# First MLP of a diffusion block: one sum on DVE placed two units later, and eight narrow matmuls of the mixer's shift spread through the next chunk

## The chip, the cores and the metric

The kernel runs on one core of a Trainium2 chip. The metric is the device time of the program in microseconds (us); the kernel before takes 1244.91 us, the median of 3 runs (1244.38 to 1244.93). The engines of the core are named as in the profile: PE (matmuls), PEld (its weight loads), DVE (vector), ACT (scalar, activations), POOL (GpSimd) and SP (the queue that issues all loads and stores).

## What is computed

Two layers of a diffusion backbone, over 512 latent tokens and 256 context tokens, 1024 wide. Layer 0 mixes tokens with pooling windows, layer 1 with attention; each is followed by an MLP with squared ReLU, 4096 wide. Every sublayer is shifted, scaled and gated by vectors that come from a conditioning vector:

```python
sh1, sc1, g1, sh2, sc2, g2 = jnp.split(s_lat @ ada_w[i] + ada_b[i], 6, axis=-1)
a_l = modulate(rms_norm(h_lat, norm_g[i, 0]), sh1, sc1)
y_l = pool_mix(a_l, pool_w[j], pool_scale[j])
h_lat = h_lat + g1[:, None, :] * y_l
m_l = modulate(rms_norm(h_lat, norm_g[i, 1]), sh2, sc2)
h_lat = h_lat + g2[:, None, :] * sq_relu_mlp(m_l, mlp_w1[i], mlp_w2[i])
```

with `modulate(h, shift, scale) = h * (1 + scale) + shift`. The change touches two pieces of layer 0: the product that gives the vectors (`s_lat @ ada_w`), and the shift `sh1` on its way through the pooling mixer.

## The kernel before

All arrays lie with features on the 128 partitions and tokens along the free axis: `h_lat` and `h_ctx` are 8 tiles of 128 features. A float32 operand of the large matmuls is split into a rounded high part and the rest, low (`hilo`, L91 to L93: a copy on ACT, a subtraction on DVE), and three products of the parts are summed. Weights come by SP into a landing tile (`raw`, two buffers) and are split from there into a tile `w`.

**The vectors of layer 0** are 12 blocks of 512 columns. `ada0_products` (L174) multiplies one block: eight matmuls (L199) of a 128x32 weight tile `s_w`, which holds the conditioning vector of both streams in its first two columns and zeros else, against 512 columns of the block. Matmul kt writes to the strip of 32 output partitions that kt mod 4 names, so four strips add up a part each. ACT copies the result to a row (L202). `ada0_done` (L205) turns the row by four transposes on PE (L208), adds the four strips on DVE (L211), adds the bias (L213) and, for blocks 8 and 9, makes the scale `am` (L161, in `ada_done`). The blocks' parts land in 7 buffers `praw`.

**The entry of the first MLP** (L716 to L780) is written in a fixed order for PE, DVE and ACT. There are 12 units, `units`: for each pair of feature tiles two latent units (512 columns) and one context unit (two tiles of 256). For a unit, `normed` multiplies by the scale and the norm (DVE: L737, or L735 for context), `moved` adds the shift and rounds to the high part (ACT: L748, or L745 and L746), `used` makes the low part (DVE: L759, or L757) and issues the unit's matmuls (PE: L764). Step u of the loop does `normed(u)`, `moved(u - 1)` and `used(u - 2)`. The scales of block 9 are read first by unit 6. At u = 1 the products of block 9 are issued, at u = 3 its row is turned and summed.

**The MLP** (`mlp`, L509) then goes through 16 chunks of 256 hidden columns, and from here a scheduler with priorities sets the order on the engines. Chunk c does its first matmuls (`m1_chunk`, L383), ACT and DVE apply the squared ReLU (`m1_done`), a hook `between(c)` runs, and then the second matmuls of chunk c - 1 (`m2_chunk`, L502): for each of 8 feature tiles 12 matmuls into a bank, from which DVE adds to `h_lat` and `h_ctx` (`add_gated`, L360). The hook is `between0` (L805): blocks 10 and 11 in chunk 0; blocks 0 and 1, which are the shift `sh1`, in chunk 1, with `rest_of_shift` behind them; and from chunk 2 on the vectors of layer 1, which DVE multiplies itself (`ada1_block`, L229 and L231). Block 10's products are written behind the entry but may be placed by the scheduler among its matmuls.

**`rest_of_shift`** (L783) adds what `sh1` contributes to `h`. The pooling mixer takes the mean over a window less the token itself, so of a shift that is the same for all tokens only its difference from itself is left: DVE writes that into `s_w` (L786), eight matmuls of a 128x32 tile and 256 columns of the pooling weights `pw` go to four strips (L791: group g to strip g), ACT copies (L793), PE turns two tiles (L796), DVE multiplies by the gate (L798), and 16 activations add the result to the 8 tiles of `h_lat` and `h_ctx` (L803). The second matmuls of chunk 1 (their first two feature tiles in banks `mm`, the next two in `aux`) stand around it.

Of the kernel before, what the change touches and what calls it, by code (L numbers as in the profile page):

```python
# [48 lines left out]
def dit_block_kernel(ctx: ExitStack, tc: tile.TileContext, xT, cols, adab, adaw, w1, w2, wqkv, wo,  # L49
# [26 lines left out]
    def new(p, shape, dt, tag, bufs=None):  # L76
        uid[0] += 1
        kw = {"bufs": bufs} if bufs else {}
        return p.tile(shape, dt, tag=tag, name=f"{tag}{uid[0]}", **kw)
# [8 lines left out]
    def ps_aux():  # L88
        return new(aux, [P, 512], F32, "aux")
# [57 lines left out]
    def load_w(src, lo_eng=dve, ring=None, raw=None):  # L147

        t = new(wp, [P, 2, 1024], F32R, "w")
        if raw is None:  # L150
            raw = new(*(ring or (raws, [P, 1024], F32, "raw")))
            nc.sync.dma_start(raw, src)
        hilo(t[:, 0], t[:, 1], raw, lo_eng)
        return t
# [8 lines left out]
    def ada_done(i, b):  # L163
        k0 = 4 * (b % 2)
        if b // 2 in (1, 4):
            a_scale(i, b // 2 // 3, k0, k0 + 4)
        if i == 0 and b // 2 == 2:
            g = pcol[:, 4, k0 : k0 + 4].unsqueeze(2).to_broadcast([P, 4, 2])
            dve.tensor_tensor(gp[:, k0 : k0 + 4], mod[0][:, 16 + k0 : 20 + k0], g, op=ALU.mult)

    def ada0_block(b):
        ada0_done(b, ada0_products(b))

    def ada0_products(b):  # L174

        ps = ps_aux()
        for u in range(4):
            if b == 7:

                if u % 2 == 0:  # L180
                    pair = new(wp, [P, 2, 1024], F32, "w")
                t = pair[:, u % 2]
                nc.sync.dma_start(t, adaw[0, b, u])
            elif (b, u) in ((5, 3), (9, 3)):

                t = new(mc, [P, 1024], F32, "mc")
                nc.sync.dma_start(t, adaw[0, b, u])
            elif b in landing:
                t = landing[b][:, u]
                nc.sync.dma_start(t, adaw[0, b, u])  # L190
            elif early:
                t = early.pop(0)
            else:
                t = new(*praw)
                nc.sync.dma_start(t, adaw[0, b, u])
            for kk in range(2):
                kt = 2 * u + kk
                o = kt % CG * (P // CG)
                pe.matmul(ps[o : o + P // CG, :512], s_w[:, kt], t[:, kk * 512 : kk * 512 + 512],  # L199
                          start=kt < CG, stop=kt >= KT - CG)  # L200
        row = new(sc, [P, 512], F32, "sc")
        act.activation(row, ps[:, :512], AF.Copy)  # L202
        return row

    def ada0_done(b, row):  # L205
        pt = ps_aux()
        for c in range(4):
            pe.transpose(pt[:, c * P : c * P + P], row[:, c * P : c * P + P], ident)  # L208
        tmp = new(sm, [P, 4, 2], F32, "sm8")
        sums = pt.rearrange("p (c j s) -> p c s j", c=4, j=CG)[:, :, :2]  # L210
        dve.tensor_reduce(tmp, sums, axis=AX.X, op=ALU.add)  # L211
        bias = bcol[:, 0, 4 * b : 4 * b + 4].unsqueeze(2).to_broadcast([P, 4, 2])
        dve.tensor_tensor(mod[0][:, 4 * b : 4 * b + 4], tmp, bias, op=ALU.add)  # L213
        ada_done(0, b)
# [37 lines left out]
    def hs(k0, k1, c0, n):  # L252

        if c0 < SEQ:
            return h_lat[:, k0:k1, c0 : c0 + n]
        return h_ctx[:, k0:k1, c0 - SEQ : c0 - SEQ + n]
# [85 lines left out]
    def step(steps):  # L342

        while steps:
            try:
                next(steps[0])
                return
            except StopIteration:
                steps.pop(0)
# [333 lines left out]
    row = ada0_products(2)  # L683
    tile0 = pool_tile(0)
    ada0_done(2, row)
    scaled(*tile0)
    scaled(*pool_tile(1))
    row = ada0_products(4)
    scaled(*pool_tile(2))
    ada0_done(4, row)  # L690
    scaled(*pool_tile(3))

    for dt in range(8):
        ps = mix(dt)
        if dt in (0, 3):
            row = ada0_products(3 + 2 * (dt > 0))
# [10 lines left out]
        if dt == 5:  # L707
            row = ada0_products(7)
# [21 lines left out]
    def normed(u):  # L730
        s, k, w = units[u]
        _, c0, n = segs[s]
        t = held[u] = new(sc, [P, w, n], F32, "sc")
        if s:
            dve.tensor_tensor(t, hs(k, k + w, c0, n), rbs[s].unsqueeze(1).to_broadcast([P, w, n]), op=ALU.mult)  # L735
        else:
            dve.scalar_tensor_tensor(t[:, 0], hs(k, k + 1, c0, n)[:, 0], am[0][1][:, k, :1], rbs[s], op0=ALU.mult, op1=ALU.mult)  # L737

    def moved(u):
        s, k, w = units[u]  # L740
        _, c0, n = segs[s]
        t, hi = held[u], ms(m, 0, slice(k, k + w), c0, n)
        if s:
            for x in range(w):
                act.activation(t[:, x], t[:, x], AF.Identity, scale=am[0][1][:, k + x, 1:2], bias=mod[0][:, 24 + k + x, 1:2])  # L745
            act.activation(hi, t, AF.Copy)  # L746
        else:
            act.activation(hi, t, AF.Identity, bias=mod[0][:, 24 + k, :1])  # L748

    def used(u):  # L750

        s, k0, w = units[u]
        _, c0, n = segs[s]
        k = slice(k0, k0 + w)
        t, hi, lo = held.pop(u), ms(m, 0, k, c0, n).bitcast(F32), ms(m, 1, k, c0, n)
        if s:
            dve.tensor_tensor(lo, t, hi, op=ALU.subtract)  # L757
        else:
            dve.scalar_tensor_tensor(lo, t, mod[0][:, 24 + k0, :1], hi, op0=ALU.add, op1=ALU.subtract)  # L759
        for k in range(k0, k0 + w):  # L760
            for wt, ps in zip(ws, pss):
                for wx in range(2):
                    for ax in range(2 - wx):
                        pe.matmul(ps[:, c0 : c0 + n], wt[:, wx, k * P : k * P + P], ms(m, ax, k, c0, n),  # L764
                                  start=k + wx + ax == 0, stop=k == KT - 1 and wx == 1)

    for u in range(len(units) + 2):
        if u < len(units):
            normed(u)
        if 0 < u <= len(units):  # L770
            moved(u - 1)
        if u > 1:
            used(u - 2)

        if u == 1:
            last = ada0_products(9)
        elif u == 3:
            ada0_done(9, last)
    ws = [load_w(w1[0, 2 + t]) for t in range(2)]
    by_hand.close()  # L780
    m1_done([act0[:, t] for t in range(2)], pss)
# [1 line left out]
    def rest_of_shift():  # L783

        rest = s_w[:, :, :2]
        dve.tensor_tensor(rest, mod[0][:, :KT], mod[0][:, :KT], op=ALU.subtract)  # L786
        ps = ps_aux()
        for kc in range(2):
            for g in range(4):
                o = g * (P // CG)  # L790
                pe.matmul(ps[o : o + P // CG, :256], s_w[:, 2 * g + kc], pw[:, 2 * g + kc], start=kc == 0, stop=kc == 1)  # L791
        row = new(sc, [P, 256], F32, "sc")
        act.activation(row, ps[:, :256], AF.Copy)  # L793
        pt = ps_aux()
        for d in range(2):
            pe.transpose(pt[:, d * P : d * P + P], row[:, d * P : d * P + P], ident)  # L796
        left = new(sm, [P, 4, 2, 2], F32, "sm16", 2)
        dve.tensor_tensor(left, pt[:, :256].rearrange("p (d g s) -> p g d s", d=2, g=4)[:, :, :, :2],  # L798
                          gp.rearrange("p (g d) s -> p g d s", d=2), op=ALU.mult)
        for k in range(KT):  # L800
            for s, c0, n in segs:
                h = hs(k, k + 1, c0, n)[:, 0]
                act.activation(h, h, AF.Identity, bias=left[:, k // 2, k % 2, s : s + 1])  # L803

    def between0(c):  # L805
        if c == 0:
            ada0_block(10)
            ada0_block(11)
        if c == 1:
            ada0_block(0)  # L810
            ada0_block(1)
            rest_of_shift()
        if 2 <= c < 14:
            beside.append(ada1_block(ADA_1[c - 2]))
            step(beside)
# [11 lines left out]
    def to_attn(c0, n):  # L827
        def place():

            if c0 not in spot:  # L830
                t = new(mc, [P, 3, n], F32, "mc") if c0 == SEQ else new(rp, [P, 3, n], F32, "r")
                spot[c0] = t[:, :2], t[:, 2]
            return spot[c0]

        def each(dt):
            if dt % 2:
                squares(place()[0] if dt > 1 else None, dt - 1, 2, c0, n, place()[0])

        def after():
            yield from norm_steps(1, 0, c0, n, lazy_m("a", True), *place())  # L840
        return (c0, n), each, after()

    last = [to_attn(SEQ, CTX), to_attn(0, 256), to_attn(256, 256)]
# [382 lines left out]
```

## Time and profile before

| What | Value |
|---|---|
| Median of 3 runs | 1244.91 us |
| Profiled execution: time | 1244.81 us |
| Profiled execution: span of the core | 1242.6 us |
| PE busy | 1218.8 us (98%) |
| DVE busy | 1020.7 us (82%) |
| ACT busy | 589.7 us (47%) |
| Clock granted to PE | 0.998 of full |

A row of the timeline reads: start in us, how long the merged row lasts, engine, line of the kernel, operation, output<-input, shape, count, and in brackets how long the engine stood before and what released it. `<-issue` means that the engine waited for nothing that the profile shows. The rows of PE overlap: a matmul's end is modelled, and the next one starts while it drains. A matmul of plain float32 that stands once in the program shows as two rows of PE and of PEld; those of split operands show as one.

### The profile page before, as it was taken

To read this page: it belongs to the slowest core of one execution; us is meant where nothing else is said; L and a number is where in the kernel's file an instruction comes from. 1 tells how busy PE (TensorE), PEld (TensorE's weight loads), DVE (VectorE), ACT (ScalarE), POOL (GpSimd) and SP (SyncE) were. 2 spreads that over 40 slices of the span, in tenths; PEclk is the share of its full clock that TensorE was granted. 3 is DMA by queue.
4 is the path that set the end of the run, shared out by engine and by line. 5 is a ranking of instruction groups with operands and counts; after the bars stand their busy time and mean duration, and the time that the engine had idled before them with its cause. 6 is when DMAs were issued, how large, how long until landed. Compare 5 with 4: busy or idle time off the path is not lost.

```text
span 1242.6 us, 19981 instructions
## 1 busy us (share of the span) xinstructions
PE 1218.8 (98%) x7884; PEld 1079.4 (87%) x7884; DVE 1020.7 (82%) x1725; ACT 589.7 (47%) x1055; POOL 143.3 (12%) x129
## 2 busy tenths in 40 slices
PE   7999999999999999999999999999999999999997
PEld 5766888899999999999988898988988999999996
DVE  6675998888989888867888388879899989898986
ACT  6464523444444444433555264554555454545443
POOL 0400000122221322231012001000000000000002
PEclk9999999999999999999999999999999999999999
DMA  9865325333434343321122020212223322223202
GB/s 349 346 241 218 125 85 161 108 104 119 153 120 136 119 135 120 120 69 34 35 94 86 18 78 26 69 35 69 102 85 102 117 105 96 108 89 116 71 32 69
DMA packets 41311, 138.64 MB, mean 112 GB/s; under 512 B 4737, under 2 KB 8065, under 8 KB 41089
## 3 DMA queue, kind: packets, MB, share of 16 engines
q1 hardware_dynamic: 41216, 137.36, 31.9%
q8 instruction: 62, 1.02, 0.3%
q14 instruction: 33, 0.26, 0.1%
HBM read 135.25 MB, written 2.10 MB: 111 GB/s over the span
## 4 chain that ended last, share of the span: by engine, by line
PE 64%; issue 27%; DVE 3%; DMA 2%; ACT 1%; POOL 1%; SPq 0%; POOLq 0%; DVEq 0%; ACTq 0%
PE aux L502 11%; PE mm L502 10%; PE aux L894 7%; PE mm L451 5%; PE aux L471 5%; PE mm L383 5%; PE aux L451 4%; PE aux L1014 3%; PE aux L1003 3%; PE mm L972 2%; PE aux L993 2%; DMA raw<-in_dram 1%; PE mm L675 1%; PE aux L199 1%; PE mm L764 1%
## 5 line engine op out<-in xcount | busy, mean ns | idle before, releaser
L502 PE MATMUL aux<-act,w 128*128 128x512 f32 (+1 forms) x1224 | 239.1, 346 | 0.3
L502 PE MATMUL mm<-act,w 128*128 128x512 f32 (+1 forms) x1224 | 237.2, 345 | 0.0
L502 PEld LDWEIGHTS mm<-act,w 128*128 128x128 f32 x1224 | 194.9, 189 | 30.6 <-issue 0.8
L502 PEld LDWEIGHTS aux<-act,w 128*128 128x128 f32 x1224 | 194.8, 189 | 29.6 <-DVE h_lat L360 0.7
L93 DVE TENSOR_TENSOR w<-raw,w 128x1024 fp32r<-128x1024 f32 x106 | 129.4, 1225 | 29.4 <-ACT w L92 29.2
L92 ACT ACTIVATE w<-raw 128x1024 fp32r<-128x1024 f32 x106 | 110.1, 1056 | 74.2 <-PE aux L502 39.6
L360 DVE SCALAR_TENSOR_TENSOR h_lat<-aux,mod,h_lat 128x512 f32<-128x512 f32 (+1 forms) x180 | 122.7, 687 | 17.5 <-PE aux L502 14.1
L440 POOL TENSOR_TENSOR sc<-pair 128x512 f32<-128x512 f32 x55 | 79.2, 1447 | 310.6 <-PE aux L247 102.1
L360 DVE SCALAR_TENSOR_TENSOR h_lat<-mm,mod,h_lat 128x512 f32<-128x512 f32 (+1 forms) x140 | 97.9, 701 | 5.8 <-PE mm L502 4.2
L383 PE MATMUL mm<-m_m_hi,w 128*128 128x512 f32 (+1 forms) x320 | 92.8, 352 | 0.2 <-ACT m_m_hi L92 0.2
L894 PE MATMUL aux<-w,a_m_hi 128*128 128x256 f32 (+1 forms) x384 | 87.3, 321 | 0.0
L231 DVE SCALAR_TENSOR_TENSOR mc<-raw,s_f,mc 128x512 f32<-128x512 f32 x112 | 83.6, 766 | 2.5 <-DMA raw<-in_dram 1.8
L451 PE MATMUL mm<-m_m_hi,mc 128*128 128x256 f32 x384 | 69.8, 281 | 0.0
L894 PEld LDWEIGHTS aux<-w,a_m_hi 128*128 128x128 f32 x384 | 63.5, 190 | 5.1
L383 PEld LDWEIGHTS mm<-m_m_hi,w 128*128 128x128 f32 x320 | 56.3, 189 | 10.2 <-ACT r L391 0.8
L471 PE MATMUL aux<-m_c,w 128*128 128x256 f32 x528 | 61.8, 276 | 0.0
L894 PE MATMUL aux<-w,a_m_lo 128*128 128x256 f32 (+1 forms) x192 | 61.2, 319 | 0.0
L471 PEld LDWEIGHTS aux<-m_c,w 128*128 128x128 f32 x528 | 61.0, 188 | 0.0
L451 PEld LDWEIGHTS mm<-m_m_hi,mc 128*128 128x128 f32 x384 | 59.5, 188 | 0.5
L298 POOL TENSOR_TENSOR sm<-sm,neghalf 128x2 f32<-128x2 f32 (+1 forms) x9 | 6.6, 738 | 443.8 <-DVE sm L296 443.8
L383 PE MATMUL mm<-m_m_lo,w 128*128 128x512 f32 (+1 forms) x160 | 56.2, 351 | 0.7 <-DVE m_m_lo L93 0.7
L451 PE MATMUL mm<-m_m_lo,mc 128*128 128x256 f32 x192 | 53.9, 281 | 0.0
(256 smaller groups left out, 2454.6 us busy)
## 6 DMA issues: line engine op xcount, KB each, us to landing
raw<-in_dram SPq DMA_DIRECT2D x155, 512.0 KB, 3.8
praw<-in_dram SPq DMA_DIRECT2D x34, 512.0 KB, 8.2
fin<-in_dram SPq DMA_DIRECT2D x24, 512.0 KB, 4.4
pair<-in_dram SPq DMA_DIRECT2D x22, 512.0 KB, 5.0
w<-in_dram SPq DMA_DIRECT2D x8, 512.0 KB, 10.2
h_lat<-in_dram SPq DMA_DIRECT2D x4, 512.0 KB, 6.1
block<-in_dram SPq DMA_DIRECT2D x4, 512.0 KB, 5.3
out_dram<-fin SPq DMA_DIRECT2D x8, 256.0 KB, 2.5
```

What stands on the lines that cost most here:

```text
L92: act.activation(hi, src, AF.Copy)
L93: lo_eng.tensor_tensor(lo, src, hi.bitcast(F32), op=ALU.subtract)
L231: dve.scalar_tensor_tensor(acc[:, s], w, scal, acc[:, s], op0=ALU.mult, op1=ALU.add)
L360: dve.scalar_tensor_tensor(h, ps, gate[:, dt, s : s + 1], h, op0=ALU.mult, op1=ALU.add)
L383: pe.matmul(ps[:, c0 : c0 + cn], lhs, ms(m, ax, k, c0, cn), start=k + wx + ax == 0, stop=k == KT - 1 and wx == 1)
L440: eng.tensor_tensor(t, x, y, op=how)
L451: pe.matmul(places[n], w[:, wx, k * P : k * P + P], inputs[n][ax][:, k], start=k + wx + ax == 0, stop=k == 3 and wx == 1)
L471: pe.matmul(pc[:, t * 256 : t * 256 + 256], ws[k // 4][:, wx, k % 4 * P : k % 4 * P + P], ms(m, ax, k, SEQ, CTX), start=k + wx + ax == 0, ...
L502: pe.matmul(ps, lhs, a[:, t, ax, c0 : c0 + n], start=t + wx + ax == 0, stop=t == 1 and wx == 1)
L894: pe.matmul(ps, lhs, ws[u][:, wx, o : o + width], start=k + ax + wx == 0, stop=k == KT - 1 and ax == 1)
L1003: pe.matmul(po, v[:, vx, k, g * HD : g * HD + HD], pT[:, px, k, j0:j1].rearrange("p j q -> p (j q)"), start=k + vx + px == 0, stop=k == 5 ...
L1014: pe.matmul(ps, ws[j][:, wx, dt * P : dt * P + P], o[ax][:, j, c0 : c0 + n], start=j + wx + ax == 0, stop=j == 1 and ax == 1)
```

## The change

Two edits. First, `ada0_done` is cut in two: the turning on PE (`ada0_turned`) stays at u = 3 of the entry, while the sums on DVE move to u = 5. Second, `rest_of_shift` is cut: the write of `s_w`, the matmuls and ACT's copy stay in chunk 1 but are given a lower priority (`offset=-40`), so that the scheduler sets them further back; the transposes, the gate and the 16 activations (`rest_added`) move to the hook of chunk 2.

```diff
-    def ada0_done(b, row):
+    def ada0_turned(row):
         pt = ps_aux()
         for c in range(4):
             pe.transpose(pt[:, c * P : c * P + P], row[:, c * P : c * P + P], ident)
+        return pt
+
+    def ada0_done(b, row, pt=None):
+        pt = pt or ada0_turned(row)
         tmp = new(sm, [P, 4, 2], F32, "sm8")
...
         elif u == 3:
-            ada0_done(9, last)
+            pt9 = ada0_turned(last)
+        elif u == 5:
+            ada0_done(9, last, pt9)
...
         row = new(sc, [P, 256], F32, "sc")
         act.activation(row, ps[:, :256], AF.Copy)
+        return row
+
+    def rest_added(row):
         pt = ps_aux()
         for d in range(2):
             pe.transpose(pt[:, d * P : d * P + P], row[:, d * P : d * P + P], ident)
...
-            rest_of_shift()
+
+            with tc.high_priority(offset=-40):
+                left_over.append(rest_of_shift())
+        if c == 2:
+            rest_added(left_over.pop())
```

What the order of the instructions shows of it, with the lines of each kernel's own file (below the edits the changed file's lines are 4 to 15 higher: L211 is L215, L764 is L768, L791 is L797, L502 is L506).

DVE at the entry of the MLP, units 3 to 6, before; `aux_826` is the turned row of block 9:

```order
L737 SCALAR_TENSOR_TENSOR sc_814<-h_lat,am_136,aux_764 128x512
L759 SCALAR_TENSOR_TENSOR m_m_lo<-sc_782,mod_132,m_m_hi 128x512
L211 TENSOR_REDUCE sm_831<-aux_826 128x8
L213 TENSOR_TENSOR mod_132<-sm_831,bcol 128x8
L161 SCALAR_TENSOR_TENSOR am_136<-mod_132,pcol 128x8
L737 SCALAR_TENSOR_TENSOR sc_835<-h_lat,am_136,aux_764 128x512
L757 TENSOR_TENSOR m_c_776<-sc_804,m_c_774 128x512
L735 TENSOR_TENSOR sc_851<-h_ctx,aux_769 128x512
L759 SCALAR_TENSOR_TENSOR m_m_lo<-sc_814,mod_132,m_m_hi 128x512
```

DVE at the same place in the changed kernel:

```order
L741 SCALAR_TENSOR_TENSOR sc_814<-h_lat,am_136,aux_764 128x512
L763 SCALAR_TENSOR_TENSOR m_m_lo<-sc_782,mod_132,m_m_hi 128x512
L741 SCALAR_TENSOR_TENSOR sc_831<-h_lat,am_136,aux_764 128x512
L761 TENSOR_TENSOR m_c_776<-sc_804,m_c_774 128x512
L739 TENSOR_TENSOR sc_847<-h_ctx,aux_769 128x512
L763 SCALAR_TENSOR_TENSOR m_m_lo<-sc_814,mod_132,m_m_hi 128x512
L215 TENSOR_REDUCE sm_857<-aux_826 128x8
L217 TENSOR_TENSOR mod_132<-sm_857,bcol 128x8
L161 SCALAR_TENSOR_TENSOR am_136<-mod_132,pcol 128x8
```

Four of the units' instructions now stand ahead of the three for block 9.

PE at the same place before, from the turning of block 9 on; `aux_982` takes the products of block 10:

```order
L764 MATMUL mm_779<-m_m_hi,w_691 128x512
L208 MATMUL aux_826<-ident,sc_802 128x128 x4
L764 MATMUL mm_778<-m_c_774,w_686 128x256
L199 MATMUL aux_982<-praw_983,s_w_146 32x512 x2
L199 MATMUL aux_982<-praw_987,s_w_146 32x512 x2
L764 MATMUL mm_778<-m_c_776,w_686 128x256
```

PE in the changed kernel some 20 matmuls further on, in unit 4, where the first of block 10's products now stands; the other seven have moved to the end of the entry, where the last four stood before:

```order
L768 MATMUL mm_779<-m_m_hi,w_691 128x512
L768 MATMUL mm_778<-m_m_hi,w_686 128x512
L199 MATMUL aux_982<-praw_983,s_w_146 32x512
L768 MATMUL mm_778<-m_m_lo,w_686 128x512
L768 MATMUL mm_778<-m_m_hi,w_686 128x512
```

The context unit is no longer cut by four products, and unit 4's matmuls are cut by one.

PE in chunk 1, where the rest of the shift is multiplied, before; `mm_1273` is the second feature tile's bank, `aux_1288` and `aux_1289` the third's:

```order
L502 MATMUL mm_1273<-act,w_1253 128x512
L502 MATMUL mm_1273<-act,w_1253 128x256
L791 MATMUL aux_1199<-pw,s_w_146 32x256 x8
L796 MATMUL aux_1210<-ident,sc_1208 128x128 x2
L502 MATMUL aux_1288<-act,w_1248 128x512
L502 MATMUL aux_1289<-act,w_1248 128x256
```

PE at the same place in the changed kernel, the first half of the third feature tile:

```order
L506 MATMUL mm_1252<-act,w_1232 128x256
L797 MATMUL aux_1199<-pw,s_w_146 32x256
L506 MATMUL aux_1267<-act,w_1227 128x512
L506 MATMUL aux_1268<-act,w_1227 128x256
L506 MATMUL aux_1267<-act,w_1227 128x512
L797 MATMUL aux_1199<-pw,s_w_146 32x256
L506 MATMUL aux_1268<-act,w_1227 128x256
L506 MATMUL aux_1267<-act,w_1227 128x512
L797 MATMUL aux_1199<-pw,s_w_146 32x256
L506 MATMUL aux_1268<-act,w_1227 128x256
L797 MATMUL aux_1199<-pw,s_w_146 32x256
L506 MATMUL aux_1267<-act,w_1232 128x512
```

The eight matmuls no longer stand in a row: one to three matmuls of the full array stand between each and the next, up to the end of this feature tile. The two transposes stand behind the last of chunk 2's first matmuls. In SP's queue the loads of block 11's last part and of block 0's first stand behind the two weight loads for chunk 1's second matmuls; before, they stood ahead of them. On DVE the write of `s_w` stands behind the first feature tile's `add_gated`, and the gate product (L798) is in chunk 2 between the first two instructions of that chunk's `ada1_block`. On ACT the 16 activations stand in chunk 2.

## What was predicted

> **What bounds the kernel now.** I read the busy times first, then the table by stages around the change, then who waits for whom on TensorE, then the timeline of the two places that are edited.
>
> ```profile
> PE 1218.8 (98%) x7884; PEld 1079.4 (87%) x7884; DVE 1020.7 (82%) x1725; ACT 589.7 (47%) x1055; POOL 143.3 (12%) x129
> ```
>
> TensorE (PE) is busy for 98% of the span, so what counts is what the change does to PE: waits that it takes away, and PE time that it adds.
>
> The next rows give the busy time of each engine (PE, weight loads, DVE, ACT, POOL) in three stretches of 30 us; both edits work between 60 and 160 us.
>
> ```profile
> 60.00:90.00 30.00, 28.78 (x191) 20.48 (x190) 23.92 (x42) 16.93 (x28) 4.27 (x4) 1.00 0.65 250
> 120.00:150.00 30.00, 28.85 (x176) 24.53 (x176) 28.75 (x43) 15.65 (x25) 0.00 (x0) 1.00 0.39 130
> 150.00:180.00 30.00, 30.00 (x175) 25.92 (x174) 29.19 (x43) 7.06 (x9) 1.31 (x1) 1.00 0.21 66
> ```
>
> PE is idle for 1.22 us in the first and for 1.15 us in the second, and full in the third; DVE has about 1 us free in 30 from 120 to 180. The waits view of PE names these gaps:
>
> ```profile
> PE mm L764 <- DVE m_c L757: 0.8, 1, 0.8
> PE aux L791 <- DVE s_w L786: 0.7, 1, 0.7
> PE aux L796 <- ACT sc L793: 0.5, 1, 0.5
> ```
>
> The change aims at these three, 2.0 us together. More than that no wait near it can give back.
>
> **Block 9's sums.** The timeline from the turning of block 9 (L208) on:
>
> ```profile
> 74.00 0.60 PE L208 MATMUL aux<-ident,sc 128*128 128x128 f32 x4
> 74.36 0.36 PE L764 MATMUL mm<-m_c,w 128*128 128x256 f32 x1
> 74.64 0.19 DVE L211 TENSOR_REDUCE sm<-aux 128x8 f32<-128x32 f32 x1 [1.96 <-PE aux L208]
> 74.65 1.06 PE L199 MATMUL aux<-praw,s_w 128*32 128x512 f32 x8
> 75.15 0.74 DVE L737 SCALAR_TENSOR_TENSOR sc<-h_lat,am,aux 128x512 f32<-128x512 f32 x1
> 76.54 1.56 PE L764 MATMUL mm<-m_c,w 128*128 128x256 f32 x11 [0.83 <-DVE m_c L757]
> 90.55 1.06 PE L199 MATMUL aux<-praw,s_w 128*32 128x512 f32 x8
> 91.55 0.50 PE L383 MATMUL mm<-m_m_hi,w 128*128 128x512 f32 x1
> ```
>
> DVE stands 1.96 us before the sums (L211), and behind it are queued L737 and then L757, whose result PE waits for. With the sums behind unit 5's L735 and unit 3's L759, L737 starts at 72.68 (74.64 - 1.96) and L757 soon after 73.4, some 2 us ahead of now, so the context group follows its first matmul at once. That first one streams for some 0.12 us from 74.36, so PE gains 76.54 - 74.48 = 2.06 us. It isn't all gain, because half of block 10's products (L199) lay in that gap, 4 of 8 matmuls. In the new order one stands alone amid unit 4's matmuls and seven stand at 90.55, where four stood. What these cost needs the price of a product matmul by itself.
>
> **The price of a lone 32-column matmul.** The weight loads (PEld) and matmuls of a batch of eight L199:
>
> ```profile
> 96.04 0.16 PEld L199 LDWEIGHTS aux<-praw,s_w 128*32 128x32 f32 x8 [0.17 <-DMA praw<-in_dram]
> 96.50 0.13 PEld L199 LDWEIGHTS aux<-praw,s_w 128*32 128x32 f32 x4 [0.30 <-issue]
> 96.92 0.13 PEld L199 LDWEIGHTS aux<-praw,s_w 128*32 128x32 f32 x4 [0.30 <-issue]
> 97.89 0.19 PEld L383 LDWEIGHTS mm<-m_m_hi,w 128*128 128x128 f32 x1 [0.84 <-issue]
> ...
> 96.04 1.93 PE L199 MATMUL aux<-praw,s_w 128*32 128x512 f32 x16
> 98.23 0.28 PE L383 MATMUL mm<-m_c,w 128*128 128x256 f32 x1
> ```
>
> Eight matmuls are 16 rows, two each, and go in rounds of four, one for each strip of 32 columns: a round takes 0.42 to 0.46, four rounds 1.72, and the next full matmul comes 1.85 after the first. So a lone matmul of 512 columns holds PE for two rounds, 0.86, as long as four side by side; one of 256 columns (L791) for 0.43. Going back to the full array costs 0.13 of drain (1.85 - 1.72), and its first weight load is not ahead: 97.89 to 98.23 is 0.34. The next rows show that L383 of 512 columns otherwise takes 0.23 (111.15 to 111.38; half of it, 0.12, for 256), so 0.11 more. Going in costs 0.09: 0.21 from the last L383, of 256 columns, to L199.
>
> ```profile
> 111.15 0.39 PE L383 MATMUL mm<-m_m_hi,w 128*128 128x512 f32 x1
> 111.38 0.28 PE L383 MATMUL mm<-m_c,w 128*128 128x256 f32 x1
> 111.59 0.64 PE L199 MATMUL aux<-praw,s_w 128*32 128x512 f32 x4
> ```
>
> A lone L791 between full matmuls then costs 0.43 + 0.09 + 0.13 + 0.11 = 0.76, a lone L199 1.19. The bounds: 0.13 if it shares the array as in a batch (1.07 for the eight L791 of now, row below), 0.43 if switching is free, 0.76 if every switch is paid. I take 0.76, because the row at 97.89 is just this switch: the full weight load stood idle 0.84 until the strips were done.
>
> The Trainium skill (TensorEngine Tiling (Array Packing), Tiling Modes, "Key Properties") says that a change of tiling mode drains TensorE; the trace agrees, with 0.13 of drain. By that rule the eight switches cost what I take, without it 0.43 each, 0.86 for the lone L199, and a total 3.0 us lower.
>
> So for block 9 and block 10: -2.06, +1.19 for the lone L199, +0.85 at 90.55 (1.85 for seven in four rounds, for 1.00). Sum 0.0. The lone L199 also covers DVE, which then has its three small sums (0.51 from L211 to L737) ahead of unit 4's L759: without that cover PE would wait up to 0.5. Bounds -1.0 (the lone one at 0.23, its share of a batch) to +0.6.
>
> **SP's queue.** The loads of block 11's last part and of block 0's first now stand behind two weight loads that wait for DVE (L93 frees their buffers):
>
> ```profile
> 62.01 14.53 SPq L195 DMA_DIRECT2D praw<-in_dram  x9
> 88.80 1.47 SPq L152 DMA_DIRECT2D raw<-in_dram  x2
> praw<-in_dram SPq DMA_DIRECT2D x16, 512.0 KB, 5.8
> praw<-in_dram SPq DMA_DIRECT2D x34, 512.0 KB, 8.2
> ```
>
> They were out by 76.54, and go now at about 89. With 5.8 us to land (the median from 60 to 130 us; 8.2 over the whole program) block 11's is there by 95, before its products' last two rounds at 96.9. I count 0, and at most 0.5 if it takes the 8.2.
>
> **The rest of the shift.** The stretch in which it stood, between PE's second and third group of chunk 1:
>
> ```profile
> 118.56 2.46 PE L502 MATMUL mm<-act,w 128*128 128x256 f32 x13
> 119.19 0.75 DVE L231 SCALAR_TENSOR_TENSOR mc<-raw,s_f,mc 128x512 f32<-128x512 f32 x1 [1.76 <-DMA raw<-in_dram]
> 121.36 0.17 DVE L786 TENSOR_TENSOR s_w<-mod 128x16 f32<-128x16 f32 x1
> 121.68 1.07 PE L791 MATMUL aux<-pw,s_w 128*32 128x256 f32 x16 [0.66 <-DVE s_w L786]
> 123.24 0.44 PE L796 MATMUL aux<-ident,sc 128*128 128x128 f32 x2 [0.49 <-ACT sc L793]
> 123.43 4.49 PE L502 MATMUL aux<-act,w 128*128 128x512 f32 x24
> 125.13 0.75 DVE L360 SCALAR_TENSOR_TENSOR h_lat<-mm,mod,h_lat 128x512 f32<-128x512 f32 x1
> 125.79 0.48 DVE L360 SCALAR_TENSOR_TENSOR h_ctx<-mm,mod,h_ctx 128x256 f32<-128x256 f32 x1
> ```
>
> The 13 L502 end their streams at 118.56 + 2.46 - 0.28 + 0.12 = 120.86 (the last row's 0.28 holds 0.12 of stream, as above). Without the step the next group would start there, so it holds PE for 123.43 - 120.86 = 2.6 us, and all of that goes. What comes:
> - Eight L791, each alone between L502: 8 x 0.76 = 6.1 (bounds 1.07 and 6.1).
> - The wait of the first for s_w stays. DVE is held by the same load until 119.19; L786 then has one pair of L360 ahead of it in place of two L231, which is some 0.3 less by the rows of L231 (0.75) and L360 (0.75 and 0.48). L791 starts near 121.4, where PE is ready at 120.95: 0.4 (bounds 0 and 0.7).
> - The two transposes (L796) at the end of chunk 2's first matmuls: four took 74.00 to 74.36, so two take 0.2. Their copy (L793) is long done there: the wait of 0.49 goes for good.
>
> Sum: -2.6 + 6.1 + 0.4 + 0.2 = +4.1.
>
> Of the later half, DVE's one sum and ACT's 16 shifts move into chunk 2. ACT's part lay beside full PE before and does again; DVE's L360 follow them one row block at a time, slower than ACT makes them:
>
> ```profile
> L803 ACT ACTIVATE h_lat<-h_lat,sm x8: 707/708/727, 123.9 to 131.0; 128x512 f32<-128x512 f32 x8
> ```
>
> That is 1.0 us between the starts of two row blocks, against 2.2 us in which PE makes one (4.49 us for the 24 L502 of two, above). I cost it at 0; the cover is what PE has in hand over DVE, and the third rival is its end.
>
> **Sum.** 0.0 + 0.0 + 4.1 = +4.1 on 1244.81 of the profiled execution (its span 1242.6), which is 0.10 under the median of 1244.91: **1248.9 us**.
>
> **The rivals.** A measurement of this kernel can tell about 0.2%, 2.5 us, from no change.
> - The full array's weights are loaded while a lone strip still streams, and drain and late load (0.13 + 0.11) vanish: 8 x 0.52 = 4.2 and 0.95 for the lone L199, the total +1.9, 1246.7. Against it stands the 0.84 at 97.89, though there four strips were streaming and not one. The Trainium skill (TensorE: Matmul & The Clock Gate, Part 2) says that loads are pulled ahead of running matmuls when they go to the background buffer; the trace shows that for full matmuls in a row, and not at 97.89. 0.17, no change.
> - Not slower: a lone strip runs beside the full matmuls as its like do beside each other, at 0.13. Then the rest of the shift costs 1.07 + 0.4 + 0.2 - 2.6 = -0.9, block 9 and 10 -2.06 + 0.23 + 0.85 = -1.0, together -1.9, 1242.9. It decides at 0.32 a matmul, the lone L199 at twice that: 10 x 0.32 is what the edits free (2.06 - 0.85 + 2.6 - 0.6). Only rounds of equal strips speak for it. 0.08: 0.05 no change, 0.03 faster.
> - DVE falls behind. Its sum of the rest (L798) now waits, with L231 and the xs and weight splits (L93) and every L360 of chunk 2 queued behind it, for transposes that PE does at the end of chunk 2's first matmuls:
>
> ```profile
> 136.40 16.64 PE mm L383 x96
> 152.54 0.48 DVE L229 TENSOR_SCALAR mc<-raw,s_f 128x512 f32<-128x512 f32 x1
> ```
>
> PE ends those at 153.04 plus the delay of 3.9; DVE is there at 152.9 if it is not delayed along. That would be up to 4 us of idle DVE, and DVE had 0.8 us free in 150 to 180: some 2 us more reach PE through late weights, 1250.9. Against it: DVE's L360 of chunk 1 wait for the same delayed matmuls, so DVE comes later too. 0.13, slower.
>
> **How the numbers follow.** The forecast gets 0.62: every price has its row, and only the lone strip was not seen. Its own range is 1247.2 (0.55 a matmul: 4.4 + 0.6 - 2.6) to 1250.3 (the wait for s_w, block 9 and the load at their upper ends: 0.3 + 0.6 + 0.5 more); below +2.5 lies about 0.05 of its chance. Slower 0.57 + 0.13 = 0.70; no change 0.05 + 0.17 + 0.05 = 0.27; faster 0.03. The range, 1245.9 to 1251.0, takes in the first and the third rival and leaves out the second.
>
> **What would show it.** Right: L757 ahead of L211 and no wait of L764 near 76; eight L791 with two rows each between L502, about 0.7 from the end of one full matmul to the next; the full weight load idle by "issue" after each; a wait of L791 for s_w under 0.7; no other new wait of PE up to 300 us. Wrong: L502 starts within 0.5 us across an L791, a stretch from 120 to 130 that is no longer than before, or PE waiting for L93 or L360 after 155.

## The result, and the profile after

The changed kernel takes 1249.34 us (median of 7 runs, 1248.09 to 1250.08), the kernel before beside it 1244.93 (7 runs, 1244.18 to 1245.36): a ratio of 1.0034, with an interval of 1.0025 to 1.0043. It is slower, by 4.4 us; the forecast was +4.1. Its profiled execution took 1250.08 us (span 1247.9, clock 0.997), the slowest of the seven. Of the 5.3 us between its span and that of before, 4.7 are there when chunk 3 begins, in the changed kernel and then in the kernel before:

```profile
174.00 0.50 PE L387 MATMUL mm<-m_m_hi,w 128*128 128x512 f32 x1
169.32 0.50 PE L383 MATMUL mm<-m_m_hi,w 128*128 128x512 f32 x1
```

The rest comes in the last 40 us or so, where this execution had a lower granted clock (0.92 from 1200 us to its end, against 0.95 in the kernel before).

The busy times by stage (PE, PEld, DVE, ACT, POOL) in two of the stretches shown of before:

```profile
60.00:90.00 30.00, 29.61 (x194) 20.80 (x196) 24.08 (x42) 17.53 (x30) 4.27 (x4) 1.00 0.59 230
120.00:150.00 30.00, 30.00 (x156) 22.27 (x155) 24.33 (x39) 4.45 (x6) 0.00 (x0) 1.00 0.39 133
```

PE's gap from 60 to 90 has shrunk from 1.22 to 0.39 and the one from 120 to 150 is gone, yet PE does less there: 156 instructions in 30 us, where it did 176. A busy PE is not a PE that gets on. The first row of PE's waits from 55 to 170 us:

```profile
PE aux L199 <- DMA praw<-in_dram: 0.6, 1, 0.6
```

The three waits that the change aimed at are all gone. A new one is there, for a load (`praw`) that PE did not wait for at this place before.

**The entry.** The timeline of PE from the turning of block 9 on:

```profile
73.89 0.60 PE L208 MATMUL aux<-ident,sc 128*128 128x128 f32 x4
74.24 1.66 PE L768 MATMUL mm<-m_c,w 128*128 128x256 f32 x12
...
76.90 0.62 PE L768 MATMUL mm<-m_m_hi,w 128*128 128x512 f32 x2
77.45 1.05 PE L199 MATMUL aux<-praw,s_w 128*32 128x512 f32 x2
78.42 0.50 PE L768 MATMUL mm<-m_m_lo,w 128*128 128x512 f32 x1
78.76 0.62 PE L768 MATMUL mm<-m_m_hi,w 128*128 128x512 f32 x2
...
89.54 1.92 PE L199 MATMUL aux<-praw,s_w 128*32 128x512 f32 x14
91.38 0.50 PE L387 MATMUL mm<-m_m_hi,w 128*128 128x512 f32 x1
```

The twelve context matmuls follow each other without a gap. From the turning to the first matmul of chunk 0 it is 91.38 - 73.89 = 17.49 us, before 91.55 - 74.00 = 17.55. What the closed gap gave, the lone product (77.45) and the seven at 89.54 have taken.

**Chunk 1.** The next rows are PE's, from block 1's products to the two feature tiles behind the third and fourth:

```profile
113.28 1.56 PE L506 MATMUL mm<-act,w 128*128 128x512 f32 x7
115.21 1.91 PE L199 MATMUL aux<-praw,s_w 128*32 128x512 f32 x12
117.76 1.05 PE L199 MATMUL aux<-praw,s_w 128*32 128x512 f32 x4 [0.64 <-DMA praw<-in_dram]
118.75 0.97 PE L506 MATMUL mm<-act,w 128*128 128x256 f32 x4
...
122.34 0.62 PE L797 MATMUL aux<-pw,s_w 128*32 128x256 f32 x2
122.89 0.85 PE L506 MATMUL aux<-act,w 128*128 128x512 f32 x3
123.67 0.62 PE L797 MATMUL aux<-pw,s_w 128*32 128x256 f32 x2
...
132.42 4.32 PE L506 MATMUL mm<-act,w 128*128 128x512 f32 x24
136.58 0.74 PE L506 MATMUL aux<-act,w 128*128 128x512 f32 x3
```

Two things are to be seen. Up to 113.28 PE is level with before (113.44). Block 1's 16 rows then take 115.21 to 118.75, 3.54 us, where the kernel before took 115.37 to 117.38, 2.01: that is 1.5 us that no step of the prediction has. Only 0.64 of it is a wait. The rest is that the late part's two products, which before stood beside the two ahead of them, now stream in two rounds of their own (0.43 each). And the 24 matmuls of the third and fourth feature tiles, with the eight L797 among them, take 132.42 - 122.34 = 10.08; the 24 of the next two take 136.58 - 132.42 = 4.16. Eight lone strips cost 5.92, 0.74 each. The first of the weight loads behind a strip:

```profile
122.89 0.53 PEld L506 LDWEIGHTS aux<-act,w 128*128 128x128 f32 x3 [0.41 <-PE mm L506]
```

It stands idle for 0.41 us until the strip has streamed, and so do those behind the next strips (0.41 each).

**Where the late load comes from.** SP's queue in the changed kernel and then in the kernel before, and ACT's split of the weight (L92) that waits for a landing tile `raw`, in the changed kernel and before:

```profile
90.61 7.99 SPq L195 DMA_DIRECT2D praw<-in_dram  x8
98.66 1.70 SPq L152 DMA_DIRECT2D raw<-in_dram  x2
111.41 0.33 SPq L226 DMA_DIRECT2D raw<-in_dram  x1
112.52 0.33 SPq L195 DMA_DIRECT2D praw<-in_dram  x1
109.06 1.06 ACT L92 ACTIVATE w<-raw 128x1024 fp32r<-128x1024 f32 x1 [3.39 <-DMA raw<-in_dram]
```

```profile
91.65 7.24 SPq L195 DMA_DIRECT2D praw<-in_dram  x6
98.98 1.11 SPq L152 DMA_DIRECT2D raw<-in_dram  x2
109.31 0.33 SPq L222 DMA_DIRECT2D raw<-in_dram  x1
106.96 1.06 ACT L92 ACTIVATE w<-raw 128x1024 fp32r<-128x1024 f32 x1 [1.13 <-DMA raw<-in_dram]
```

Eight loads of 512 KB go out around 95 us instead of six, so the first of the weight loads behind them, issued 0.3 us sooner than before, lands 2.1 us later (ACT reads it at 109.06 against 106.96). The tile they land in is free 2.1 us later, so the load of L226 goes out at 111.41 in place of 109.31, only 1.1 us ahead of block 1's last part (112.52), where it was 3.4. That part's time from issue to landing, in the changed kernel and then in the kernel before:

```profile
praw<-in_dram SPq DMA_DIRECT2D x1, 512.0 KB, 5.2
praw<-in_dram SPq DMA_DIRECT2D x1, 512.0 KB, 3.7
```

Issued at 112.52 and 112.68, it lands at about 117.7 and 116.4, and PE goes on 1.0 us behind each landing (118.75 and 117.38). The two extra loads are those whose buffers block 10's first four products read: these products stood at 74.65 and stand at 89.54 now.

### The profile page after: what moved, and what is told of

It reads as the page before. It is cut to its first block, busy times and chain, and to the rows that moved or that the text cites. A ratio compares the mean times of both kernels' runs of the same rounds, so it can differ in the third digit from the quotient of the medians.

```text
span 1247.9 us, 19980 instructions
## 1 busy us (share of the span) xinstructions
PE 1224.8 (98%) x7884; PEld 1079.8 (87%) x7884; DVE 1021.8 (82%) x1725; ACT 588.9 (47%) x1055; POOL 143.3 (11%) x129
## 4 chain that ended last, share of the span: by engine, by line
PE 66%; issue 27%; DVE 3%; ACT 1%; DMA 1%; POOL 1%; SPq 0%; POOLq 0%; DVEq 0%; ACTq 0%
PE aux L506 11%; PE mm L506 10%; PE aux L909 7%; PE mm L387 5%; PE mm L455 5%; PE aux L475 5%; PE aux L455 4%; PE aux L1029 3%; PE aux L1018 3%; PE mm L987 2%; PE aux L1008 2%; PE aux L199 2%; PE mm L679 1%; PE mm L768 1%; PE mm L988 1%
## 5 line engine op out<-in xcount | busy, mean ns | idle before, releaser
L506 PE MATMUL aux<-act,w 128*128 128x512 f32 (+1 forms) x1224 | 241.0, 346 | 0.3
L506 PE MATMUL mm<-act,w 128*128 128x512 f32 (+1 forms) x1224 | 237.2, 345 | 0.2 <-ACT w L92 0.2
L506 PEld LDWEIGHTS aux<-act,w 128*128 128x128 f32 x1224 | 195.0, 189 | 32.6 <-issue 2.9
L506 PEld LDWEIGHTS mm<-act,w 128*128 128x128 f32 x1224 | 194.8, 189 | 30.9 <-ACT w L92 1.4
L92 ACT ACTIVATE w<-raw 128x1024 fp32r<-128x1024 f32 x106 | 110.1, 1056 | 90.1 <-PE aux L506 39.4
```

Source lines behind the costliest of these rows:

```text
L92: act.activation(hi, src, AF.Copy)
L506: pe.matmul(ps, lhs, a[:, t, ax, c0 : c0 + n], start=t + wx + ax == 0, stop=t == 1 and wx == 1)
```

## The experiments

The theory is that two prices make up the +4.4: the lone strips, because each makes PE change the shape of its tile and back, and the two late loads, which the first edit causes through block 10's products. The rivals are that any lone float32 matmul costs this much; that the late landing was chance; and that the work added in chunk 2 costs something by itself. Line numbers differ by a few between the kernels (L506 is L508 in some); the operands tell which is which. Two numbers follow each run: the median against the kernel before beside it (1245.20 for the first four, 1245.08 for the last four), and in its profile the time that block 1's 16 rows take until the next matmul.

| Kernel | Median us | Against before | Ratio, interval | 16 rows, us |
|---|---|---|---|---|
| before | 1244.93 | | | 2.01 |
| changed | 1249.34 | +4.4 | 1.0034 (1.0025, 1.0043) | 3.54 |
| full array | 1246.64 | +1.4 | 1.0012 (1.0003, 1.0021) | 2.85 |
| one batch | 1244.68 | -0.5 | 0.9994 (0.9985, 1.0003) | 2.92 |
| sums alone | 1245.04 | -0.2 | 0.9999 (0.9990, 1.0008) | 2.60 |
| rest alone | 1248.77 | +3.6 | 1.0030 (1.0018, 1.0041) | 2.12 |
| four by hand | 1247.98 | +2.9 | 1.0021 (1.0012, 1.0030) | 2.01 |
| batch amid chunk 1 | 1244.30 | -0.8 | 0.9992 (0.9983, 1.0001) | 2.80 |
| both mended | 1243.03 | -2.1 | 0.9982 (0.9973, 0.9990) | 1.90 |
| pairs | 1245.91 | +0.8 | 1.0007 (0.9998, 1.0016) | 2.60 |

**Full array.** The changed kernel, the eight L797 at the same places, but over the whole array:

```diff
-                o = g * (P // CG)
-                pe.matmul(ps[o : o + P // CG, :256], s_w[:, 2 * g + kc], pw[:, 2 * g + kc], start=kc == 0, stop=kc == 1)
+                z = s_w[:, 4 * kc : 4 * kc + 4].rearrange("p k s -> p (k s)")
+                pe.matmul(ps[:, :256], z, pw[:, 2 * g + kc], start=kc + g == 0, stop=kc + g == 4)
```

> The changed kernel, with each of the eight lone matmuls of the rest of the shift (L797) done over all 128 columns of weights in place of 32, with zeros as weights (the rest then comes out as zero, so that the output lacks it). Places, streams and loads stay. Theory: of the change's +4.4 us some 3.3 come from the lone matmuls, and they cost 0.74 each because TensorE goes to a tile of 32 columns and back; at full width only the stream of 0.43 and little more is left, so 8 x (0.74 - 0.45) = 2.3 us go: about 1247.0, +2.1 on the kernel before (1244.9). Rival: any float32 matmul amid the others costs this much, whatever its tile: 1249.3 as the changed kernel.

PE's timeline of this run at the same place, the first of the eight and the end:

```profile
122.19 0.59 PE L797 MATMUL aux<-pw,s_w 128*128 128x256 f32 x2
122.43 0.94 PE L506 MATMUL aux<-act,w 128*128 128x512 f32 x3
...
130.01 4.32 PE L506 MATMUL mm<-act,w 128*128 128x512 f32 x24
```

From the first to the fifth feature tile it is 130.01 - 122.19 = 7.82, less 4.16 for the 24 others: 3.66, 0.46 each, against 0.74 as strips. The median is 2.7 under the changed kernel, 3.0 counted against the kernel before beside each; 2.3 had been expected from the theory and nothing from the rival, which falls. Why 0.7 more went than expected is not shown. Of the 0.74 of a strip 0.43 is its stream, and 0.3 is the change of shape, there and back, with the weight load that stands idle behind it.

The Trainium skill (TensorEngine Tiling (Array Packing), Tiling Modes, "Key Properties") says that a change of tiling mode, not of the tile alone, drains TensorE. Full array against strips at the same places agrees with it, with 0.28 us a time (0.74 - 0.46).

**One batch.** The changed kernel without the priority, so that the eight stand side by side:

```diff
-            with tc.high_priority(offset=-40):
-                left_over.append(rest_of_shift())
+            left_over.append(rest_of_shift())
```

> The changed kernel without the priority that spreads the eight L797: they stand side by side as one batch, as before the change; transposes, sum and shifts stay a chunk later, and block 9's sums stay behind unit 5. Theory: the batch costs its four rounds and one switch (1.07 + 0.24) in place of 5.9 us, so 4.5 go at that place, of which the wait for s_w takes back up to 0.7: 1245.2 to 1245.9, +0.3 to +1.0 on the kernel before, the rest being the late loads of block 10's landing buffers (+1.4) less the wait for the copy and the two transposes (-0.7). Rival that the chain in chunk 2 (sum and 16 shifts beside the next block's work) is what costs: 1247 or more.

The time is 1244.68, 0.5 under the kernel before, where at least 0.3 over it had been expected: the 1.4 put down for the late loads was too much (the 16 rows take 0.9 more than before), and part of that only fills the wait for `s_w`, which is 0.30 here. The sum and the 16 activations in chunk 2 cost nothing that can be seen, and this rival falls.

**Sums alone.** Only the first edit; the last lines of the hook are as before:

```diff
-            with tc.high_priority(offset=-40):
-                left_over.append(rest_of_shift())
-        if c == 2:
-            rest_added(left_over.pop())
+            rest_added(rest_of_shift())
```

> Only the first half of the change: block 9's sums behind unit 5; the rest of the shift whole and in one batch in chunk 1, as before. Theory: block 10's first four products now stand 14 us later, so two landing buffers come free 14 us later, their two loads of 512 KB go out amid the other loads of 90 to 108 us, and a weight load and block 1's last part land some 2 us late: TensorE is 1.2 to 1.5 us late at 119 us: 1246.2, between +0.9 and +1.5 on the kernel before. Rival: the late landing in the changed kernel is chance and has nothing to do with block 9: 1244.9, within 0.4 of the kernel before.

The time says the rival (-0.2, the interval reaches from -1.2 to +1.0), but the profile says the theory:

```profile
115.41 2.66 PE L199 MATMUL aux<-praw,s_w 128*32 128x512 f32 x16
...
119.19 2.46 PE L506 MATMUL mm<-act,w 128*128 128x256 f32 x13
121.57 1.07 PE L797 MATMUL aux<-pw,s_w 128*32 128x256 f32 x16
```

PE is 0.63 late at 119.19 (118.56 before), and the batch at 121.57 starts even ahead of the one before (121.68), because it has no wait for `s_w` any more: the 0.66 us that PE stood there before now cover the delay. The theory's expectation missed that. It was also too high by itself: the 16 rows take 0.6 more here and not 1.5.

**Rest alone.** Only the second edit; block 9's sums at unit 3:

```diff
-            pt9 = ada0_turned(last)
-        elif u == 5:
-            ada0_done(9, last, pt9)
+            ada0_done(9, last)
```

> Only the second half of the change: eight lone L797 and the rest added a chunk later; block 9's sums behind unit 3 as before. Theory: loads stay early, so TensorE is not late at 119 us; the rest of the shift costs 5.9 + 0.2 for 2.6, and up to 0.7 more for s_w: 1248.2, +3.3 (2.9 to 4.0) on the kernel before. Rival, no effect of the loads: the whole +4.4 stands here, 1249.3.

It takes +3.6, within the theory's bounds, though the interval (2.2 to 5.1) does not shut out the rival's 4.4; the profile tells them apart. The loads are early and the 16 rows short again; and the first L797 now waits:

```profile
115.52 2.19 PE L199 MATMUL aux<-praw,s_w 128*32 128x512 f32 x16
117.64 0.97 PE L506 MATMUL mm<-act,w 128*128 128x256 f32 x4
...
121.72 0.59 PE L795 MATMUL aux<-pw,s_w 128*32 128x256 f32 x2 [0.42 <-DVE s_w L790]
```

So the late loads and the wait for `s_w` are alternatives: who is late for the one reason does not wait for the other.

**Four by hand.** The changed kernel, with four of block 10's products issued at unit 4:

```diff
-    def ada0_products(b):
+    def ada0_products(b, ps=None, us=range(4)):
...
+        elif u == 4:
+            ps10 = ada0_products(10, us=range(2))
...
-            ada0_block(10)
+            ada0_done(10, ada0_products(10, ps10, range(2, 4)))
```

> The changed kernel, with four of block 10's eight products issued as one batch behind unit 4's sums at the entry, in place of the lone one; the other four stay ahead of chunk 0. The eight L797 stay alone. Theory: the first two landing buffers are free again at about 78 us, their loads go out far ahead of the full stretch from 90 us, the weight load and block 1's last part land as in the kernel before, and the 16 products ahead of 118 us take 2.0 us again (3.5 in the changed kernel's profile, 2.6 and 2.9 in the runs with the loads late so far); block 10's products take 2.3 in place of 2.8. Together some 1.1 us under the changed kernel: 1248.2, +3.0 on the kernel before. Rival, the late landing has another cause than those buffers: the 16 products still take 2.6 or more, 1248.8 to 1249.3.

+2.9 (1.5 to 3.7), where the theory had +3.0. SP's queue, ACT's split and PE of this run:

```profile
64.27 14.65 SPq L195 DMA_DIRECT2D praw<-in_dram  x7
90.96 7.24 SPq L195 DMA_DIRECT2D praw<-in_dram  x6
106.34 1.06 ACT L92 ACTIVATE w<-raw 128x1024 fp32r<-128x1024 f32 x1 [1.19 <-DMA raw<-in_dram]
76.19 1.07 PE L199 MATMUL aux<-praw,s_w 128*32 128x512 f32 x8
77.19 0.50 PE L770 MATMUL mm<-m_m_hi,w 128*128 128x512 f32 x1
114.69 2.08 PE L199 MATMUL aux<-praw,s_w 128*32 128x512 f32 x16
116.70 0.98 PE L508 MATMUL mm<-act,w 128*128 128x256 f32 x4
```

The loads are out by 79 us, six follow at 91, the weight is there at 106.34, and the 16 rows take 2.01. With it the last column of the table is whole: the four kernels whose two loads go out early take 1.90 to 2.12, the six in which they go out at 91 us take 2.60 to 3.54. The delay is the first edit's, 0.6 to 0.9 in five profiles and 1.5 in one; how much it is in one run depends on when block 1's last part lands. In all ten profiles PE goes on 1.0 us behind that landing, and from issue to landing the part took 3.6 to 3.8 us in the four kernels, 4.3 to 4.6 in five of the six, and 5.2 in the changed one. In the four the load of L226 went out 3.3 to 3.4 us ahead of it, and took 3.5 to 3.6 itself, so that it was all but there; in the six it went out 0.4 to 2.2 us ahead and was still under way. The rival of chance falls for the delay, not for its size.

**Batch amid chunk 1**, and **both mended**. The first issues the eight by hand behind the third feature tile, through the hook `each` of `m2_chunk`; the second is that and four by hand together:

```diff
+    def amid(dt):
+        if dt == 2:
+            left_over.append(rest_of_shift())
...
+                         each=amid if between and c == 1 else None)
...
-            with tc.high_priority(offset=-40):
-                left_over.append(rest_of_shift())
```

> The changed kernel, with the eight L797 as one batch behind the third feature tile of chunk 1's second product, where s_w has long been there; the rest is added in chunk 2 as in the change. Theory: one switch for all eight, 1.07 + 0.24 = 1.3 us in place of 5.9, and no wait for s_w or the copy: 4.6 under the changed kernel, 1244.7, within 0.7 of the kernel before; the late loads of block 10 stay in it. Rival, that the work added in chunk 2 costs something by itself: over 1246.

> The two edits before this one together: four of block 10's products as a batch at the entry, and the eight L797 as one batch amid chunk 1. Theory: what the change aimed at without its two costs, some 1.1 us under the run with the batch alone: 1243.6, -1.5 (-0.8 to -2.0) on the kernel before. Rival, TensorE's gains here are taken back by DVE, which has no room from 120 to 180 us: no faster than the batch alone, 1244.7.

PE's timeline of both mended:

```profile
121.96 1.07 PE L802 MATMUL aux<-pw,s_w 128*32 128x256 f32 x16
...
125.18 4.40 PE L508 MATMUL mm<-act,w 128*128 128x512 f32 x24
129.42 4.40 PE L508 MATMUL aux<-act,w 128*128 128x512 f32 x24
```

The next 24 matmuls take 4.24 here (in other places, and around the lone strips, 4.16). The eight cost 125.18 - 121.96 - 2.12 (half of 4.24) = 1.10 us as a batch. Both runs came out as the theory expected, a little lower: 1244.30, and 1243.03 together. The first is not told apart from the kernel before (its interval reaches 1.0001). The second is faster than the kernel before, 0.9982 with an interval of 0.9973 to 0.9990, and beats both kernels of this case. That DVE takes the gain back is not seen.

**Pairs.** As the batch amid chunk 1, but two strips at a time, one pair behind each of four feature tiles:

```diff
+                if g % 2:
+                    yield
...
+        if 2 <= dt < 7:
+            next(pairs[0], None)
```

> The run with the batch amid chunk 1, but the eight L797 in four pairs, two strips of 32 columns side by side, one pair behind each of the feature tiles 2 to 5. Theory: a pair streams in one round and pays one switch, as a lone strip does, 0.74: 4 x 0.74 = 3.0 us in place of 1.3, so 1.7 over the batch (1246.4, +1.2 on the kernel before) and 2.9 under the changed kernel. Rival, the price is by matmul and not by switch: 5.9 as in the changed kernel, 1249.3.

PE's timeline of this run, the first pair and the last:

```profile
123.50 0.63 PE L797 MATMUL aux<-pw,s_w 128*32 128x256 f32 x4
...
132.10 0.63 PE L797 MATMUL aux<-pw,s_w 128*32 128x256 f32 x4
132.66 4.51 PE L506 MATMUL aux<-act,w 128*128 128x512 f32 x24
```

From 123.50 to 132.66 stand four pairs and 36 matmuls of the full array (6.24 to 6.36, at 4.16 to 4.24 for 24): 2.80 to 2.92, 0.70 to 0.73 a pair. A pair costs about what a lone strip costs, so the price goes by switches: 5.9 for eight, 2.9 for four, 1.1 for one. Taking off 0.43 for each round of stream (eight, four and two rounds) leaves 0.31, 0.27 to 0.30, and 0.24 a switch. The median is 1.6 above the batch amid chunk 1, where the theory had 1.7, and 3.4 under what the rival had.

## Why the prediction came out right, and which step failed

- **Block 9 and block 10, 0.0**: right, -0.06. The lone L199 was costed at 1.19; it took 78.42 - 76.90 - 0.47 (two matmuls at 0.235) = 1.05, and the next full one came 0.11 late (0.34 to 78.76 in place of 0.23), 1.16 in all. Seven products in four rounds took 1.84, for 1.85.
- **SP's queue, 0, at most 0.5**: this step failed. The prediction asked whether the two loads that go later are there in time for their own products, and they are. (They go at about 91, when block 10's products give their buffers free, and not at 89.) It did not ask what they collide with at 91 us. Two loads more in front of the weight loads moved a chain of three (a weight lands late, its tile is free late, the next load goes late) up to the one load that PE waits for, which then took 5.2 us to land in place of 3.7. It cost 1.5 in the profiled execution and 0.6 to 0.9 in five other kernels with the same loads.
- **Rest of the shift, +4.1**: the eight strips took 5.9 in place of 6.1, and the price of 0.76 was right to 0.02, with its two parts, stream and change of shape. The wait for `s_w`, 0.4, is 0.42 in the run with the second edit alone, 0.21 in the run with four by hand, and nothing in the changed kernel, since PE arrives late there. So this step's 0.4 and the failed step are two sides of one thing, and they work against each other: -0.2 and -0.4 here, and there 1.5 in the changed kernel's profile (4.7 late at chunk 3 for the 4.1) and 0.6 to 0.9 in the five others. How large the delay is in a median execution no profile shows. That the sum of 4.1 comes so near to 4.4 is in this part luck: the price of the strips was right, and a term at nothing and a term that did not come nearly cancel.
- **The later half, 0**: right. The 16 activations run from 160.2 to 168.6 beside a full PE.
- **The first rival**, loads pulled ahead of a lone strip, is wrong by the 0.41 of idle load after each. **The second**, a strip that runs beside full matmuls at 0.13, is wrong too, since each took 0.74. Of **the third**, a DVE that falls behind, a wait of 0.24 for a weight at 194 us can be seen at most (24 matmuls take 4.72 there in place of 4.24). It is not shown to be DVE's, and the run with one batch has such a wait too, of 0.41, and no loss; the changed kernel is 4.7 late far behind this place (951.77 against 947.07) as it was ahead of it.

Open stays why block 1's last part took 5.2 us to land in the changed kernel's profile and 4.3 to 4.6 in the five others with the same loads. The distance to the load of L226 ahead of it does not order them: 1.1 us in the changed kernel, 0.4 in the one with the full array, where it took 4.5.

## What to carry to other kernels

Count how often TensorE changes the shape of its tile, not how many narrow matmuls there are: strips that stand together share one stream and one switch, and a strip set alone into a gap of a wait pays both every time, so that even a wait of 0.7 us for a batch is cheaper than eight lone strips. When a reader of a landing buffer moves later, its next load moves too: look where that load goes out now, what else is in flight there, and which load that pushes back. And a wait that goes may only have been the cover of another delay, so two edits are costed together and not one by one.

## What was not expected of the hardware

A single float32 matmul over the full array, with other weights before and behind it, costs 0.46 us for 256 columns, hardly more than the 0.43 that its stream as a strip takes: to change the weights alone is nearly free, to change the shape is not. And with the same loads in the same order one load of 512 KB took from 4.3 to 5.2 us to land, and the 16 rows behind it from 2.60 to 3.54.
